# Four chunks of 264 columns in place of three of 352 in a hybrid attention layer's projections

## The chip, the cores and the metric

The kernel runs on one core of a Trainium2 chip. The metric is the device time of one execution in microseconds. Besides the timed runs there is one profiled execution, whose trace gives the start and duration of each instruction on each engine: TensorE (PE, with its weight loads as PEld), VectorE (DVE), ScalarE (ACT), GpSimd (POOL) and the DMA queues.

## What is computed

One layer of a streaming encoder, for 1024 new frames and 32 frames of a running stream (1056 columns in all), with a model width of 1024 in float32. Cut to what matters:

```
u  = rmsnorm(x) @ w_in                       # eleven slices: gq gk gv gr gg dq dk dv dg ma mb
o_gla  = gated linear attention, 4 heads     # gq gk gv and the decay from gr
o_diff = p1 @ v - lam * p2 @ v, 8 heads      # two softmaxes over rotated dq, dk; v = dv
yg = rmsnorm(o_gla)  * silu(gg)
yd = rmsnorm(o_diff) * (1 - lambda_init) * silu(dg)
merged = sigmoid(ma) * (yg @ w_proj_gla) + sigmoid(mb) * (yd @ w_proj_diff)
y = x + rmsnorm(merged @ w_out)
```

Returned are y, the new rows of k and v, and the new linear-attention states, each for the new frames and for the running stream.

## The kernel before

Every float32 operand is split into a high and a low part, and a product is three matmuls: high by high, low by high, high by low. The kernel goes through these stages, in this order of time.

Values (to 214 us): x is normed, and the slices gv and dv are made with 512 columns at a time.

Linear attention (240 to 600 us) and softmax attention (600 to 1183 us): all other slices of the input projection are made here, with features in the rows and the 1056 frames in the columns. Such a projection is a job: 128 output features, whose 128 x 1024 weights are loaded by DMA, rounded to the high part on ACT (L433) and split on POOL (L435). A job works in chunks of columns. A chunk takes one of two banks of the kind `pj` and runs 8 x 3 matmuls into it (L465 to L467); then ACT or DVE reads the bank out: a tanh into a gate (L484), a tanh and a product for a SiLU (L477, L478), a copy into q or k of a linear head (L496) or of a softmax head (L806). There are 56 such jobs. They are the filling work: the attention heads' own steps come first wherever their inputs are there, and the jobs fill the time between.

What comes when on TensorE is set before the program runs by a small planner (class `Order`). Each thread of work yields steps with a cost in us, the events that it needs with a latency, and the banks that it takes. The planner goes through time, always takes the first thread in its list whose step is ready, and writes that step's matmuls. The filling thread yields a step every two of the eight k (six matmuls). On the other engines the scheduler orders the work, and evacuations are placed early (`high_priority`).

First merge (1183 to 1286 us): yg @ w_proj_gla, eight jobs. Two are written by hand in L1087 to L1109 and hold six banks at once, three chunks each; the other six go through the filling thread, with the evacuation L1082 on DVE. Meanwhile DVE scales the softmax heads' results.

Second merge (1286 to 1378 us): yd @ w_proj_diff, eight jobs by `proj` (L443 to L445), each chunk followed by L1152, L1153 and L1155 on DVE and L1154 on ACT.

Output (1378 us to the end): merged @ w_out in four quarters of 256 columns (L1193 to L1195), the last norm and the stores.

Of the kernel before, what the change touches and what calls it, by code (L numbers as in the profile page):

```python
# [23 lines left out]
T = NP + NS  # L24
# [6 lines left out]
EPS = 1e-6  # L31
WC = 352
CHUNKS = [(c * WC, WC) for c in range(T // WC)]
TAU = 16.0
GATE_LIM = 60.0
LAM_INIT = 0.8 - 0.6 * math.exp(0.0)
# [12 lines left out]
N = {"fin": 1, "rr": 3, "q": 2, "k": 4, "fill": 2, "first": 200, "evac": 1200, "lead": 2}  # L49
# [73 lines left out]
def hybrid_step_kernel(ctx: ExitStack, tc: tile.TileContext, a):  # L123
# [15 lines left out]
    def bank(name):  # L139
        return pp.tile([P, 512], F32, tag="pj", bufs=2, name=name)  # L140
# [134 lines left out]
    def value_mm(i, wh, wl, meanwhile=lambda: None):  # L275
        ps = bank("ps_v")
        if i == NQ:
            sample_mm(ps, xsm, wh, wl)
            return ps
        t0 = i * P  # L280
        for k in range(KT):
            if k == 2:
                meanwhile()
            xk = xs[k]
            mm(ps, xk[:, 0, t0 : t0 + P], wh[:, k, :], start=(k == 0), stop=False)  # L285
            mm(ps, xk[:, 1, t0 : t0 + P], wh[:, k, :], start=False, stop=False)  # L286
            mm(ps, xk[:, 0, t0 : t0 + P], wl[:, k, :], start=False, stop=(k == KT - 1))  # L287
        return ps
# [22 lines left out]
    def gate_rank(wgs):  # L311
        for t0, n in CHUNKS:
            ps = bank("ps_gr")
            for k in range(KT):
                mm(ps[0:48, :n], wgs[:, k, :], xs[k][:, 0, t0 : t0 + n], start=(k == 0), stop=(k == KT - 1))
                if k < KT - 1:
                    mm(ps[0:16, :n], wgs[:, k, 0:16], xs[k][:, 1, t0 : t0 + n], start=False, stop=False)
                if k == KT - 2:
                    mm(ps[0:16, :n], wgs[:, k + 1, 0:16], xs[k + 1][:, 1, t0 : t0 + n], start=False, stop=False)
            g1 = v1.tile([16, WC], F32, tag="xr", bufs=2, name="g1")  # L320
            act(g1, ps[32:48, :n], AF.Copy)
            g2 = v1.tile([16, WC], F32, tag="xr", bufs=2, name="g2")
            ve.tensor_tensor(g2, ps[0:16, :n], g1, op=ALU.add)
            act(gst[0:16, t0 : t0 + n], g2, AF.Copy)
            act(gst[64:80, t0 : t0 + n], g2, AF.Copy)
            ve.tensor_tensor(gst[32:48, t0 : t0 + n], g2, gst[0:16, t0 : t0 + n].bitcast(F32), op=ALU.subtract)
# [3 lines left out]
    with tc.manual_schedule(engines={E.PE, E.Activation, E.DVE, E.Pool}):  # L330
# [25 lines left out]
        ps = bank("ps_v")  # L356
# [17 lines left out]
        for i in range(1, NQ + 1):  # L374
# [10 lines left out]
            ps = value_mm(i, *wv, meanwhile)  # L385
# [43 lines left out]
    def wtile(b):  # L429
        wr = wp.tile([P, KT, P], F32, tag="wr", bufs=1, name="wr")  # L430
        dma(wr, a["w128"][b])
        wh = odd(wp, KT, P, tag="wh", name="wh")
        act(wh, wr, AF.Copy)  # L433
        wl = odd(wp, KT, P, tag="wl", name="wl")
        nc.gpsimd.tensor_tensor(wl, wr, wh.bitcast(F32), op=ALU.subtract)  # L435
        return wh, wl

    def proj(w, src, evac):
        wh, wl = w
        for t0, n in CHUNKS:  # L440
            ps = bank("ps_w")
            for k in range(KT):
                mm(ps[:, :n], wh[:, k, :], src[k][:, 0, t0 : t0 + n], start=(k == 0), stop=False)  # L443
                mm(ps[:, :n], wl[:, k, :], src[k][:, 0, t0 : t0 + n], start=False, stop=False)  # L444
                mm(ps[:, :n], wh[:, k, :], src[k][:, 1, t0 : t0 + n], start=False, stop=(k == KT - 1))  # L445
            evac(ps[:, :n], slice(t0, t0 + n))

    def fill(jobs, src):

        w = wtile(jobs[0][0])  # L450
        for ji, (b, event, begin, needs) in enumerate(jobs):
            wh, wl = w
            evac = done = None
            for t0, n in CHUNKS:
                ps = None
                for k in range(KT):
                    if k % N["fill"] == 0:
                        yield 0.45 * N["fill"], (needs if ps is None else []), (["pj"] if ps is None else [])
                        if evac is None:
                            if ji + 1 < len(jobs):  # L460
                                w = wtile(jobs[ji + 1][0])
                            evac, done = begin()
                        if ps is None:
                            ps = bank("ps_w")
                    mm(ps[:, :n], wh[:, k, :], src[k][:, 0, t0 : t0 + n], start=(k == 0), stop=False)  # L465
                    mm(ps[:, :n], wl[:, k, :], src[k][:, 0, t0 : t0 + n], start=False, stop=False)  # L466
                    mm(ps[:, :n], wh[:, k, :], src[k][:, 1, t0 : t0 + n], start=False, stop=(k == KT - 1))  # L467
                with tc.high_priority(offset=N["evac"]):
                    evac(ps[:, :n], slice(t0, t0 + n))
                S.free("pj", W["w_pj"])  # L470
            done()
            S.mark(event)
# [32 lines left out]
    def gla_prep(h):  # L505
# [3 lines left out]

        for t0, n in CHUNKS:  # L510
            yield 0.15, [], ["s"]
# [20 lines left out]
        fl = gp.tile([1, 1], I32, tag="fl", name="fl")  # L532
        ve.tensor_scalar(fl, f1, -TAU * GATE_LIM, None, op0=ALU.is_lt)
        S.free("t", W["pf_t"])
        act(t1, b, AF.Exp, scale=1.0 / TAU)
        ve.tensor_scalar(t2, b, -TAU * GATE_LIM, None, op0=ALU.max)
        act(t2, t2, AF.Exp, scale=-1.0 / TAU)
        yield 0.05, [(("q", h), W["gq"]), (("k", h), W["gk"])], []
# [36 lines left out]
    def gla_exact(h):  # L575
# [3 lines left out]
        with tc.If(flag > 0):  # L579
            for li, half in enumerate(LEVELS + [0]):  # L580
                mask = gp.tile([P, P], F32, tag="sm", name="mask")
                dma(mask, a["masks"][li])
                if half:
# [6 lines left out]
                    for dst, i0, i1, src in ((e1, bv, ref, q), (e2, ref, bv, k)):  # L590
                        dv = dst[:, :ncol].rearrange("p (c s) -> p c s", s=blk)
                        ve.tensor_tensor(dv, i0, i1, op=ALU.subtract)
                        ve.tensor_scalar(dst[:, :ncol], dst[:, :ncol], 0.0, None, op0=ALU.min)
                        act(dst[:, :ncol], dst[:, :ncol], AF.Exp, scale=1.0 / TAU)
                        ve.tensor_tensor(dst[:, :ncol], dst[:, :ncol], src[:, :ncol], op=ALU.mult)
# [13 lines left out]
    def gla_head(h):  # L609
# [9 lines left out]
        bv = b[:, 0:NP].rearrange("p (c s) -> p c s", s=P)  # L619
        act(eb[:, 0:8], bv[:, :, P - 1], AF.Exp, scale=1.0 / TAU)  # L620
        act(eb[:, 8:9], b[:, T - 1 : T], AF.Exp, scale=1.0 / TAU)
# [133 lines left out]
    with tc.manual_schedule(engines=PE):  # L755
        left = S.run([[gla_thread(), None, first], [prep_thread(), None, nullcontext],
                      [fill(jobs, xs), None, nullcontext]],
                     until=lambda: ("on", GH - 1, 1) in S.at and jobs[-1][1] in S.at)
# [279 lines left out]
    for h in range(-1, DH):  # L1038
        need = [(("qk", h - 1), 0.0)] if h >= 1 else []
        n = GATES_DIFF[h + 1]  # L1040
# [8 lines left out]
    with tc.manual_schedule(engines=PE):  # L1049
        left = S.run(left + [[diff_main(), None, first], [sample_thread(), None, nullcontext],  # L1050
                             [fill(jobs, xs), None, nullcontext]],
                     until=lambda: ("pv", DH - 1, 3) in S.at and jobs[-1][1] in S.at)
# [27 lines left out]
    def pg_evac(j):  # L1080
        def evac(ps, sl):
            ve.scalar_tensor_tensor(tha[j][:, sl], tha[j][:, sl], 1.0, ps, op0=ALU.add, op1=ALU.mult)  # L1082
        return evac

    def pg_first():
# [5 lines left out]
        for j, k in sorted(((j, k) for j in range(2) for k in range(KT)), key=lambda e: (e[1] + N["lead"] * e[0], e[0])):  # L1091
# [4 lines left out]
            wh, wl = w[j]  # L1096
            for n, (t0, cw) in enumerate(CHUNKS):
                ps = b[j * 3 + n]
# [3 lines left out]
            if k == KT - 1:  # L1102
                with tc.high_priority(offset=N["evac"]):
                    for n, (t0, cw) in enumerate(CHUNKS):
                        pg_evac(j)(b[j * 3 + n][:, :cw], slice(t0, t0 + cw))
# [38 lines left out]
    for j in range(KT):  # L1144
        th = ld("thb")
        dma(th, thd[1, j])
        pt = ld("ptl")
        dma(pt, ptd[j])
        y = yp.tile([P, 2, T], F32R, tag=f"y{j}", name=f"m{j}")

        def evac(ps, sl, th=th, pt=pt, y=y):
            ve.scalar_tensor_tensor(th[:, sl], th[:, sl], 1.0, ps, op0=ALU.add, op1=ALU.mult)  # L1152
            ve.tensor_tensor(pt[:, sl], pt[:, sl], th[:, sl], op=ALU.add)  # L1153
            act(y[:, 0, sl], pt[:, sl], AF.Copy, scale=0.5)  # L1154
            ve.scalar_tensor_tensor(y[:, 1, sl], pt[:, sl], 0.5, y[:, 0, sl].bitcast(F32), op0=ALU.mult, op1=ALU.subtract)  # L1155
        proj(wtile(BLK_PD + j), yd, evac)
        mg.append(y)
# [26 lines left out]
    for u in range(4):  # L1184
        wh, wl = cw[u]
        csl = slice(u * 256, u * 256 + 256)
        for i in range(NQ + 1):
            t0 = i * P
            w = P if i < NQ else NS
            ps = (bank, dbank)[i % 2]("ps_c")[:, 0:256]  # L1190
# [110 lines left out]
```

## Time and profile before

| what | value |
|---|---|
| median of three runs | 1486.3 us (1482.65 to 1487.47) |
| profiled execution | 1483.59 us, its span 1481.9 us |
| TensorE matmuls | 8848 records, busy 1422.6 us (96%) |
| DVE, ACT, POOL busy | 786.6 us, 601.0 us, 298.4 us |
| mean granted clock of TensorE | 0.99 |

Matmuls are pipelined: one starts long before the other has ended, and their ends are modelled. So the distance between the starts of two neighbours tells what one costs, and the busy time doesn't. A row of a group gives the line, the engine, the operation, output and inputs, the shape and the count, then busy time and mean duration, then the idle time just before and what ended it. A row of a timeline gives the start, the duration and, in brackets, the idle time before and its releaser.

### The profile page before, as it was taken

Reading aid. Unit: us, or ns where it says so; the run is one execution under the profiler, and the core shown is the slowest. Engines: PE = TensorE matmul, PEld = TensorE weight load, DVE = VectorE, ACT = ScalarE, POOL = GpSimd, SP = SyncE. Lnnn points to the kernel's source line nnn. Section 1 sums busy time; section 2 is a strip of 40 time slices with the busy share of each in tenths; the row PEclk is TensorE's granted clock in tenths of the full one; section 3 lists DMA queues with packets and bytes.
Section 4 is the critical chain, followed back from the end, with each engine's and each line's share of the span. In section 5 each row is a group of like instructions: output and inputs, shape, how many; then the busy total and the mean of one; then the engine's idle time right before and its main releaser. Section 6 shows DMA issues by size and latency. Waiting matters only on the chain.

```text
span 1481.9 us, 22365 instructions
## 1 busy us (share of the span) xinstructions
PE 1422.6 (96%) x8848; PEld 1327.6 (90%) x8848; DVE 786.6 (53%) x1464; ACT 601.0 (41%) x1262; POOL 298.4 (20%) x186
## 2 busy tenths in 40 slices
PE   8999999989999999899999999999899899999997
PEld 6787789889989899899989998998899799999997
DVE  5702005755565343576767767678665535455415
ACT  5612114535344232455555555555455432221311
POOL 1200002222213224123222222222221111122001
PEclk9999999999999999999999999999999999999999
DMA  8621111122222233323232333223322278633205
GB/s 310 205 105 38 45 45 48 56 74 68 81 70 73 70 120 108 90 62 106 72 108 60 106 86 96 69 83 90 92 68 81 97 264 302 223 131 129 103 1 192
DMA packets 66742, 156.58 MB, mean 106 GB/s; under 512 B 10008, under 2 KB 28568, under 8 KB 65600
## 3 DMA queue, kind: packets, MB, share of 16 engines
q1 hardware_dynamic: 66624, 155.01, 32.3%
q8 instruction: 74, 1.21, 0.3%
q14 instruction: 44, 0.36, 0.1%
HBM read 104.39 MB, written 40.04 MB: 97 GB/s over the span
## 4 chain that ended last, share of the span: by engine, by line
PE 51%; DVE 6%; DMA 4%; ACT 2%; issue 1%; POOL 1%; SPq 0%; DVEq 0%; POOLq 0%; ACTq 0%
PE ps_w L465 9%; PE ps_w L466 9%; PE ps_w L467 9%; PE ps_w L444 2%; PE ps_w L443 2%; PE ps_w L445 2%; PE ps_s L884 2%; PE ps_t L931 2%; PE ps_s L883 2%; DMA ydr<-ydd 2%; PE ps_c L1193 2%; PE ps_c L1195 2%; PE ps_c L1194 2%; PE po L945 1%; PE po L946 1%
## 5 line engine op out<-in xcount | busy, mean ns | idle before, releaser
L465 PE MATMUL ps_w<-X,wh 128*128 128x352 f32 x1344 | 453.8, 338 | 8.5 <-DVE sg L478 3.2
L466 PE MATMUL ps_w<-X,wl 128*128 128x352 f32 x1344 | 438.2, 326 | 0.0
L467 PE MATMUL ps_w<-X,wh 128*128 128x352 f32 x1344 | 436.4, 325 | 0.0
L435 POOL TENSOR_TENSOR wl<-wr,wh 128x1024 fp32r<-128x1024 f32 x72 | 179.5, 2493 | 661.8 <-ACT wh L433 528.6
L465 PEld LDWEIGHTS ps_w<-X,wh 128*128 128x128 f32 x1344 | 255.8, 190 | 13.6 <-issue 4.9
L466 PEld LDWEIGHTS ps_w<-X,wl 128*128 128x128 f32 x1344 | 256.1, 191 | 1.2 <-issue 1.2
L467 PEld LDWEIGHTS ps_w<-X,wh 128*128 128x128 f32 x1344 | 255.1, 190 | 0.0
L889 ACT ACTIVATE p<-ps_s,nm 128x256 f32<-128x256 f32 (+7 forms) x128 | 94.6, 741 | 59.1 <-DVE ps_s L885 31.1
L286 PE MATMUL ps_v<-wh,X 128*128 128x512 f32 x248 | 97.6, 393 | 0.6 <-DVE X L225 0.6
L287 PE MATMUL ps_v<-wl,X 128*128 128x512 f32 x248 | 98.0, 395 | 0.0
L433 ACT ACTIVATE wh<-wr 128x1024 fp32r<-128x1024 f32 x72 | 75.9, 1054 | 54.6 <-PE ps_w L467 30.4
L285 PE MATMUL ps_v<-wh,X 128*128 128x512 f32 x248 | 97.9, 395 | 0.0
L887 DVE TENSOR_REDUCE nm<-ps_s 128x1 f32<-128x256 f32 (+7 forms) x128 | 94.8, 747 | 2.7
L272 DVE TENSOR_TENSOR vo<-ps_v,vo 32x512 f32<-32x512 f32 x4 | 2.7, 679 | 139.9 <-ACT vo L271 139.9
L885 DVE MEMSET ps_s<- 64x64 f32 x128 | 14.3, 112 | 115.8 <-PE ps_s L884 114.2
L650 POOL TENSOR_TENSOR vl<-vr,vh 128x512 fp32r<-128x512 f32 (+1 forms) x20 | 24.8, 1242 | 222.8 <-DVE t L516 160.3
L883 PE MATMUL ps_s<-k,q 128*128 128x512 f32 (+2 forms) x192 | 68.0, 362 | 1.2 <-DMA k<-k 1.2
L884 PE MATMUL ps_s<-kl,q 128*128 128x512 f32 (+2 forms) x192 | 63.8, 348 | 3.9 <-DMA kl<-kl 3.4
L268 ACT ACTIVATE vo<-ps_v 128x512 f32<-128x512 f32 x32 | 19.1, 596 | 114.2 <-PE ps_v L287 113.8
L933 ACT ACTIVATE ah<-ps_t 128x512 fp32r<-128x512 f32 (+2 forms) x96 | 46.9, 488 | 43.6 <-PE ps_t L931 43.0
L934 DVE TENSOR_TENSOR al<-ps_t,ah 128x512 fp32r<-128x512 f32 (+2 forms) x96 | 53.1, 554 | 18.6 <-ACT ah L933 17.3
L444 PE MATMUL ps_w<-Y,wl 128*128 128x352 f32 x192 | 62.2, 324 | 0.0
(319 smaller groups left out, 2960.9 us busy)
## 6 DMA issues: line engine op xcount, KB each, us to landing
wr<-w SPq DMA_DIRECT2D x72, 512.0 KB
thd<-gate SPq DMA_DIRECT2D x16, 528.0 KB
xn<-xn SPq DMA_DIRECT2D x16, 512.0 KB
wr<-wv SPq DMA_DIRECT2D x16, 512.0 KB
newk<-rr SPq DMA_DIRECT2D x8, 528.0 KB
ygr<-ygd SPq DMA_DIRECT2D x8, 528.0 KB
tha<-thd SPq DMA_DIRECT2D x8, 528.0 KB
ydr<-ydd SPq DMA_DIRECT2D x8, 528.0 KB
```

The source lines that it names most:

```text
L285: mm(ps, xk[:, 0, t0 : t0 + P], wh[:, k, :], start=(k == 0), stop=False)
L286: mm(ps, xk[:, 1, t0 : t0 + P], wh[:, k, :], start=False, stop=False)
L287: mm(ps, xk[:, 0, t0 : t0 + P], wl[:, k, :], start=False, stop=(k == KT - 1))
L435: nc.gpsimd.tensor_tensor(wl, wr, wh.bitcast(F32), op=ALU.subtract)
L444: mm(ps[:, :n], wl[:, k, :], src[k][:, 0, t0 : t0 + n], start=False, stop=False)
L465: mm(ps[:, :n], wh[:, k, :], src[k][:, 0, t0 : t0 + n], start=(k == 0), stop=False)
L466: mm(ps[:, :n], wl[:, k, :], src[k][:, 0, t0 : t0 + n], start=False, stop=False)
L467: mm(ps[:, :n], wh[:, k, :], src[k][:, 1, t0 : t0 + n], start=False, stop=(k == KT - 1))
L883: mm(ps[:, n0 : n0 + n], qs[m][:, qsl], ks[m][:, n0 : n0 + n], start=True, stop=False)
L884: mm(ps[:, n0 : n0 + n], qs[m][:, qsl], kls[m][:, n0 : n0 + n], start=False, stop=True)
L887: ve.tensor_reduce(nm, ps[:, 0:w], axis=AX.X, op=ALU.max, negate=True)
L889: act(p[:, 0:w], ps[:, 0:w], AF.Exp, bias=nm, accum_out=sm[:, m : m + 1])
```

## The change

A second list of chunks is added, four of 264 columns, and used in three places: in `proj` (the second merge), in the filling thread (all 56 jobs of the two attention stages and six jobs of the first merge), and in the planner's cost of a filling step, which becomes 0.35 us for each k where it was 0.45. The old list stays in use for the gate's rank projection, for the linear heads' decay, and for the two jobs of the first merge that are written by hand. Evacuations take the width from the chunk.

```diff
 WC = 352
 CHUNKS = [(c * WC, WC) for c in range(T // WC)]
+
+NC = 264
+COLS = [(c * NC, NC) for c in range(T // NC)]
@@
     def proj(w, src, evac):
         wh, wl = w
-        for t0, n in CHUNKS:
+        for t0, n in COLS:
             ps = bank("ps_w")
@@
             evac = done = None
-            for t0, n in CHUNKS:
+            for t0, n in COLS:
                 ps = None
                 for k in range(KT):
                     if k % N["fill"] == 0:
-                        yield 0.45 * N["fill"], (needs if ps is None else []), (["pj"] if ps is None else [])
+                        yield 0.35 * N["fill"], (needs if ps is None else []), (["pj"] if ps is None else [])
```

Line numbers of the changed kernel are three higher than before from here on.

The order of ACT's work in the first head of linear attention, before. L535, L620, L621 and L537 are exponentials of the head's summed decay, L496 reads out a chunk of q or k, L433 rounds weights.

```order
L496 ACTIVATE q<-ps_w 128x352
L433 ACTIVATE wh<-wr 128x1024
L535 ACT_TABLE_LOAD
L535 ACTIVATE t_1481<-b 128x1056
L620 ACTIVATE eb<-b 128x8
L621 ACTIVATE eb<-b 128x1
L537 ACTIVATE t_1482<-t_1482 128x1056
L496 ACTIVATE k<-ps_w 128x352
L545 ACTIVATE qh<-t_1481 128x1056
L496 ACTIVATE k<-ps_w 128x352 x2
```

The same place in the changed kernel:

```order
L499 ACTIVATE q<-ps_w 128x264
L436 ACTIVATE wh<-wr 128x1024
L538 ACT_TABLE_LOAD
L538 ACTIVATE t_1481<-b 128x1056
L623 ACTIVATE eb<-b 128x8
L624 ACTIVATE eb<-b 128x1
L540 ACTIVATE t_1482<-t_1482 128x1056
L499 ACTIVATE k<-ps_w 128x264
L548 ACTIVATE qh<-t_1481 128x1056
L499 ACTIVATE k<-ps_w 128x264 x3
```

The first chunk of k stands behind the same exponentials in both; it is smaller, and three follow it in place of two.

The order of TensorE's work at the end of softmax attention, before. L931 are transposes of the last head, L944 to L946 its last products, L1006, L1018, L1019 and L1029 belong to the running stream's frames, L1099 to L1101 are the first merge.

```order
L1006 MATMUL ps_st<-ident,p 32x128
L1018 MATMUL po_s<-vcs,smp 32x128 x4
L1019 MATMUL po_s<-smp 32x128
L931 MATMUL ps_t<-ident,p 128x128 x8
L1018 MATMUL po_s<-vcs,smp 32x128 x4
L1019 MATMUL po_s<-smp 32x128
L944 MATMUL po<-ah,vh 128x256
...
L946 MATMUL po<-ah,vl 128x128
L1029 MATMUL ps_so<-ident,os__13006 128x64
L1099 MATMUL ps_w<-y_13072,wh 128x352
```

In the changed kernel, from the last product of the last head on (L862 sums its squares):

```order
L949 MATMUL po<-ah,vl 128x128
L1009 MATMUL ps_st<-ident,p 128x128 x4
L468 MATMUL ps_w<-X_88,wh 128x264
...
L862 MATMUL ps_m<-sqo,one_h 128x512
L1009 MATMUL ps_st<-ident,p 32x128
L468 MATMUL ps_w<-X_89,wh 128x264
...
L862 MATMUL ps_m<-sqo,one_h 128x512
L470 MATMUL ps_w<-X_89,wh 128x264
L1102 MATMUL ps_w<-y_14528,wh 128x352
```

The last head's products come before the end of the filling work now, so 18 matmuls of it and two sums stand between them and the merge; the two groups of four transposes, which were one row of eight, have 24 matmuls of filling work between them.

## The prediction

> **What bounds the kernel now.** I read the page first, then the busy time by stage, then the starts of single matmuls.
>
> ```profile
> span 1481.9 us, 22365 instructions
> PE 1422.6 (96%) x8848; PEld 1327.6 (90%) x8848; DVE 786.6 (53%) x1464; ACT 601.0 (41%) x1262; POOL 298.4 (20%) x186
> PE 51%; DVE 6%; DMA 4%; ACT 2%; issue 1%; POOL 1%; SPq 0%; DVEq 0%; POOLq 0%; ACTq 0%
> ```
>
> TensorE is busy nearly all the time and holds most of the chain that ended last. The profiled execution took 1483.6 us around its span of 1481.9; the median of the runs is 1486.3, which is 2.7 more. The sum below is made against 1483.6, and 2.7 is added at its end.
>
> ```profile
> core 0: us, PE busy (x) PEld busy (x) DVE busy (x) ACT busy (x) POOL busy (x), PEclk, DMA share, GB/s
> 240.00:600.00 360.00, 339.46 (x2173) 325.99 (x2173) 186.47 (x312) 146.66 (x295) 97.19 (x57) 0.99 0.26 80
> 600.00:1183.00 583.00, 565.76 (x3628) 534.89 (x3628) 395.25 (x784) 301.65 (x695) 140.02 (x66) 0.99 0.28 84
> 1213.00:1285.60 72.60, 70.77 (x434) 69.19 (x433) 35.72 (x39) 18.07 (x19) 14.59 (x6) 1.00 0.75 269
> 1285.60:1378.30 92.70, 92.70 (x578) 92.70 (x577) 47.07 (x71) 19.59 (x32) 18.61 (x14) 1.00 0.39 131
> ```
>
> These are the stages that the change touches: the linear-attention stage (240 to 600), the softmax-attention stage (600 to 1183), the rest of the first merge (1213 to 1286) and the second merge (1286 to 1378). In each TensorE leaves little open and DVE and ACT have room. So what counts first is how far apart the starts of two matmuls lie, then the few places where TensorE waits.
>
> A matmul's own duration (338 ns on the page) overlaps its neighbours', so I take the distance of starts, where nothing else runs between. The rows give an operation, its count, its durations, and its first and last start.
>
> ```profile
> L443 PE MATMUL ps_w<-Y,wh x192: 318/323/326, 1285.7 to 1377.9; 128*128 128x352 f32 x192
> L1193 PE MATMUL ps_c<-cwh,m x64: 276/276/284, 1378.4 to 1399.8; 128*128 128x256 f32 x64
> L1193 PE MATMUL ps_c<-C,m x64: 281/282/285, 1402.0 to 1424.5; 128*128 128x256 f32 x64
> L1193 PE MATMUL ps_c<-C,m x64: 276/276/276, 1426.7 to 1448.1; 128*128 128x256 f32 x64
> L1193 PE MATMUL ps_c<-C,m x64: 276/276/276, 1450.2 to 1471.7; 128*128 128x256 f32 x64
> ```
>
> L443 is the first of three matmuls of 352 columns: 92.2 us over 191 triples is 482.7 ns a triple, 160.9 ns a matmul. L1193 is the first of three of 256 columns: 21.4 us over 63 triples is 113.2 ns a matmul in the first and third quarter of that stage, 113.8 in the fourth, and 22.5 us gives 119.0 in the second. Same shape, same stage, other tiles: where the operands lie moves a matmul of 256 columns by 6 ns. Per column that is 0.442 to 0.465 ns; the 352 wide ones take 0.457.
>
> **The matmuls.** How many there are:
>
> ```profile
> L465 PE MATMUL ps_w<-X,wh 128*128 128x352 f32 x1344 | 453.8, 338 | 8.5 <-DVE sg L478 3.2
> L465 PE MATMUL ps_w<-y,wh 128*128 128x352 f32 x144 | 47.1, 327 | 1.8 <-DVE tha L1082 1.8
> ```
>
> With the 192 of L443 this is 1680, in three passes and three chunks, so 1680 groups of three matmuls of 352 columns (5040) become 1680 groups of four of 264 (6720). The columns stay the same. Break-even is 482.7 / 4 = 120.7 ns a matmul.
>
> No row has 264 columns. From below: the best 256 wide pace by the column, 113.2 x 264/256 = 116.7 ns. From above: the worst, 119.0 x 264/256 = 122.7. In money: 4 x 116.7 - 482.7 = -15.9 ns x 1680 = -26.7 us; 4 x 122.7 - 482.7 = +8.1 ns x 1680 = +13.6 us. Weight loads could be a floor under this:
>
> ```profile
> 703.69 0.19 PEld L945 LDWEIGHTS po<-al,vh 128*128 128x128 f32 x1
> 703.80 0.19 PEld L946 LDWEIGHTS po<-ah,vl 128*128 128x128 f32 x1
> 703.91 0.19 PEld L465 LDWEIGHTS ps_w<-X,wh 128*128 128x128 f32 x1
> ```
>
> Behind matmuls of 128 columns they follow each other at 110 ns, so 264 columns still cover one, by 7 ns at the best pace. I take 119.5 ns, near the middle of the two ends since 264 is nearer to 256 than to 352 and half-way between good and bad tiles: 478.0 - 482.7 = -4.7 ns x 1680 = **-7.9 us**, between -26.7 and +13.6.
>
> The Trainium skill, TensorE: Matmul & The Clock Gate, section Back-to-back issue gap, gives N / 2.4 + 2.5 ns between matmuls at full clock, so every matmul pays a fixed 2.5. By it 352 columns take 149.2 and 264 take 112.5, and the group grows by 2.4 ns: an estimate of +4 us where I have -7.9. The trace puts 352 columns at 160.9, so the size of the rule isn't met here; its sign is a rival below.
>
> **Late evacuations.** A chunk's bank is one of two, and it comes free when ACT (or DVE) has read it. Two chunks cover a late one: 7.72 us of matmuls now, 48 x 119.5 ns = 5.74 after. In the first head of linear attention that cover is too short already:
>
> ```profile
> 229.92 0.32 PE L465 MATMUL ps_w<-X,wh 128*128 128x352 f32 x1
> 237.47 0.32 PE L467 MATMUL ps_w<-X,wh 128*128 128x352 f32 x1
> 240.95 0.66 PE L465 MATMUL ps_w<-X,wh 128*128 128x352 f32 x1 [3.16 <-ACT k L496]
> 231.03 5.89 DVE L524 TENSOR_TENSOR_SCAN b<-ones,t 128x128 f32<-128x128 f32 x9
> 237.00 1.28 ACT L535 ACT_TABLE_LOAD   x1 [5.46 <-DVE b L524]
> 240.45 0.44 ACT L496 ACTIVATE k<-ps_w 128x352 f32<-128x352 f32 x1
> 240.90:244.30 3.40, 3.35 (x12) 3.35 (x13) 1.26 (x1) 1.32 (x2) 0.00 (x0) 0.56 0.00 0
> PE ps_w L465 <- ACT k L496: 3.2, 1, 3.2
> PE ps_w L465 <- DVE sg L478: 3.2, 3, 1.9
> ```
>
> The job k starts at 229.9, fills two banks by 237.6, and waits until ACT, which sat behind an exponential that waits for nine scans on DVE, reads the first. With 264 columns the two banks are full at 235.7 while ACT is free at the same time: 2.0 us more. Behind the waiting matmul in TensorE's queue stands the rest of job k, and the head's score products wait for that. The last two rows are the waits view of 214 to 600: four such waits, 6.4 us. A wait that begins in a bank's first chunk grows by two chunks' difference (2.0), in its second by one (1.0). So four waits cost +2 (the first alone) to +8, and as many that just fit now could appear, up to +14. I take **+7**. The row of 240.90 shows the clock at 0.56 for the 3.4 us behind that stall; a stall longer than that is inside the +14.
>
> **Switches and ACT's work.** When TensorE comes back from transposes to the filling work, its first matmul takes longer:
>
> ```profile
> 920.42 0.41 PE L465 MATMUL ps_w<-X,wh 128*128 128x352 f32 x1
> 920.67 0.32 PE L466 MATMUL ps_w<-X,wl 128*128 128x352 f32 x1
> 920.83 0.32 PE L467 MATMUL ps_w<-X,wh 128*128 128x352 f32 x1
> ```
>
> 0.25 us to the next start, not 0.16. The order of TensorE leaves the filling work 232 times before and 247 times after (the step is shorter): 15 x 0.09 = **+1.3 us**, 0 to +2. Evacuations are more and shorter:
>
> ```profile
> L484 ACT ACTIVATE gate<-ps_w 128x352 f32<-128x352 f32 x48 | 22.2, 462 | 61.7 <-PE ps_w L467 61.6
> L947 ACT ACTIVATE sqo<-po 128x256 f32<-128x256 f32 x32 | 12.2, 380 | 41.3 <-PE po L946 38.1 <-issue 3.2
> ```
>
> Three of 462 ns become four of about 387 (an estimate between both rows): 0.16 us a job, 9 us of ACT over the 56 jobs of the two attention stages, where matmuls run beside it and ACT is busy half the time. I cost it at nothing; were none of it hidden, it would be +9. The weights' DMAs and their conversion stay one to a job. The planner's cost of a step (0.70 us for six matmuls, where 6 x 119.5 is 0.72; it was 0.90 for 0.97) puts dependent steps 4% closer in real time; 0, between -5 and +5.
>
> **The end of softmax attention.** The new order places the last head earlier against the filling work, as the rows of TensorE's order show. Now:
>
> ```profile
> 1174.38 0.66 PE L931 MATMUL ps_t<-ident,p 128*128 128x128 f32 x4
> 1176.45 0.66 PE L931 MATMUL ps_t<-ident,p 128*128 128x128 f32 x4 [1.41 <-DVE al L934]
> 1183.47 0.43 PE L1099 MATMUL ps_w<-y,wh 128*128 128x352 f32 x1 [1.51 <-ACT y L1069]
> 1184.99 0.43 PE L1101 MATMUL ps_w<-y,wh 128*128 128x352 f32 x1 [0.93 <-DVE y L1070]
> 1191.24 0.43 PE L1101 MATMUL ps_w<-y,wh 128*128 128x352 f32 x1 [0.63 <-DVE y L1070]
> ```
>
> Eight transposes follow each other with the one bank between them, and the first merge starts right behind the last products, whose tiles its own inputs need. That is 4.5 us of waits. After, a chunk of 24 matmuls (2.9 us) stands between the two groups of transposes, and 18 matmuls and two sums stand before the merge. I take **-4**, between -4.5 and 0.
>
> **Sum.** -7.9 + 7 + 1.3 - 4 = -3.6: 1480.0 for the profiled execution, 1482.7 for the median.
>
> **The rivals.** (1) Good tiles. All paces lie near the lower end, 117.2 ns: 468.8 - 482.7 = -13.9 ns x 1680 = -23.4, with the other terms (+4.3) -19: 1467. For it: three of the four quarters of L1193 run at 113.2 to 113.8. Against it: the 352 wide matmuls, whose tiles are the ones read here, do not reach 0.442 ns a column.
>
> (2) A fixed cost per matmul: slower. By the best column, 352 x 0.442 = 155.7 ns; the measured 160.9 is 5.2 more. If these 5.2 belong to each matmul of this kind, whatever its width, then 264 x 0.442 + 5.2 = 121.9, 4.9 ns over a group, +8.2 us, and with +4.3: 1498.8. It decides from 120.7 ns on. For it: the excess sits on these operands. Against it: 256 wide ones have three quarters with none. The page named above has such a fixed cost, of 2.5.
>
> (3) The banks: slower. If not four but ten evacuations come too late, in the linear stage and in the first merge where DVE's scaling stands before them, ten times 2.0 is +20 in place of 7: -7.9 + 20 + 1.3 - 4 = +9.4, 1495.7. It decides from about six such waits of 2 us each. Against it: in the softmax stage chunks are broken up by other steps, so their cover is longer.
>
> **How the numbers follow.** My forecast has 0.40, with 1478 to 1489 as its own range; (1) 0.22, (2) 0.25, (3) 0.13. About 0.3% (4.5 us) is what a measurement of this kernel can tell from no change. The forecast lies near that border: 0.20 of it counts as faster, 0.16 as no change, 0.04 as slower. With (1) all faster, (2) 0.22 slower and 0.03 the same, (3) 0.09 slower and 0.04 the same, it is faster 0.42, same 0.23, slower 0.35. The range of 1464 to 1503 takes in (1), (2) and (3) and leaves out both ends of the pace together with their worst waits.
>
> **What would show it.** In the second merge L443 has 256 rows from first to last start: 91.4 us at 119.5 ns, 92.3 at break-even, 93.3 at 121.9. The wait on the evacuation of k in the first head: 5 us, not 3.2. The waits of the first merge on y: under 1 us, and none between the last transposes. A pace over 122.7 or under 116.7, or a new wait of more than 5 us in the softmax stage, makes the prediction wrong.

## The result and the profile after

The changed kernel is slower: 1561.2 us, median of four runs (1553.2 to 1562.22), where the kernel before takes 1485.8 beside it (four runs, 1482.65 to 1487.47). The ratio is 1.050, with an interval of 1.047 to 1.054. The forecast was 1482.7 with a range up to 1503, so the time lies far outside it. The profiled executions show the same: a span of 1551.4 us against 1481.9, 69.5 more. The profiled execution is the quickest of the changed kernel; the others took 1561 to 1562 us at a mean clock of 0.969 to 0.973 where it had 0.978, so its trace shows 69.5 of the 75 us.

The head of the page of the changed kernel, its shares of the chain that ended last, and one of its costliest groups:

```profile
span 1551.4 us, 25835 instructions
PE 1448.4 (93%) x10528; PEld 1353.1 (87%) x10528; DVE 792.3 (51%) x1510; ACT 607.9 (39%) x1326; POOL 302.6 (20%) x186
PE 47%; DVE 9%; DMA 4%; ACT 3%; issue 2%; POOL 1%; SPq 0%; DVEq 0%; POOLq 0%; ACTq 0%
L887 PE MATMUL ps_s<-kl,q 128*128 128x512 f32 (+2 forms) x192 | 65.3, 354 | 23.6 <-DMA kl<-kl 23.6
```

TensorE was busy 96% of the span and is busy 93% now, while DVE's and ACT's busy times rose by 6 and 7 us only. So no other engine has become the bound; TensorE stands still more often. The last row tells the main place: L887 is the second of the products that make a softmax head's scores, it reads kl, the low part of the rounded k, and it had to wait 23.6 us in all until a DMA had brought kl.

Where the time went by stage. These are the two attention stages, the first merge and the second merge of the changed kernel; a row gives the window, its length, the busy time (and count) of PE, PEld, DVE, ACT and POOL, the granted clock, the DMA share and GB/s:

```profile
240.00:1252.00 1012.00, 927.66 (x7104) 883.95 (x7104) 583.30 (x1113) 456.39 (x1044) 236.26 (x120) 0.97 0.25 77
1252.00:1354.40 102.40, 98.86 (x743) 95.32 (x742) 48.45 (x59) 32.17 (x37) 21.54 (x9) 1.00 0.74 268
1354.40:1447.50 93.10, 93.10 (x767) 93.10 (x767) 53.73 (x97) 20.77 (x41) 18.59 (x14) 1.00 0.41 133
```

The first two of these stages in the kernel before (the prediction shows the third):

```profile
240.00:1183.40 943.40, 905.22 (x5801) 860.87 (x5801) 582.12 (x1096) 448.70 (x991) 237.21 (x122) 0.99 0.27 82
1183.40:1285.60 102.20, 98.12 (x580) 94.17 (x581) 47.90 (x52) 31.46 (x33) 16.98 (x7) 0.98 0.75 266
```

The two merges take what they took (102.4 for 102.2, 93.1 for 92.7). Of the 69.5 us, 68.6 lie in the attention stages: 1012.0 for 943.4. There TensorE's open time went from 38.2 to 84.3 us, which is 46 more, and its busy time rose by 22. The matmuls' own pace is some 5 us of that (below); the rest fits the clock, which was granted at 0.97 there and had been at 0.99, but was not measured apart.

What ended TensorE's waits, in the changed kernel (total us, times, the longest):

```profile
PE ps_s L887 <- DMA kl<-kl: 23.6, 12, 4.0
PE ps_t L934 <- DVE ps_s L888: 9.6, 5, 2.2
PE ps_kt L636 <- DVE k L628: 9.1, 4, 2.7
PE po L703 <- DVE o_sb L712: 7.6, 8, 2.1
PE ps_s L886 <- DMA k<-k: 6.0, 4, 2.5
PE ps_w L468 <- DVE sg L481: 5.6, 3, 2.1
PE ps_w L468 <- ACT k L499: 4.7, 1, 4.7
PE ps_w L468 <- ACT q L499: 1.9, 1, 1.9
PE ps_w L468 <- DVE tha L1085: 1.6, 2, 1.0
```

The same waits before (those on sg and k are in the prediction):

```profile
PE po L700 <- DVE o_sb L709: 4.1, 5, 1.5
PE ps_s L884 <- DMA kl<-kl: 3.4, 3, 2.2
PE ps_w L465 <- DVE tha L1082: 1.8, 4, 0.9
PE ps_kt L633 <- DVE k L625: 1.8, 2, 1.2
PE ps_s L883 <- DMA k<-k: 1.2, 1, 1.2
PE ps_t L931 <- DVE ps_s L885: 0.9, 3, 0.3
```

The wait on k's and kl's DMA grew from 4.6 to 29.6 us, 25 of the 46. Then come the transposes behind a head's scores (L934, +8.7), the transposes of k in the linear heads (L636, +7.3), evacuations (8.2 to 13.8, +5.6) and the linear heads' products (L703, +3.5). Only the evacuations are waits that the prediction had its eye on; the other four of the five stand outside the filling work that was changed.

One softmax head shows the largest. The row of ACT is the evacuation of the head's last chunk of k, the first row of PE its first score product. Changed kernel:

```profile
913.18 0.39 ACT L809 ACTIVATE rr<-ps_w 128x264 f32<-128x264 f32 x1 [0.23 <-PE ps_w L470]
927.63 1.17 SPq L842 DMA_DIRECT2D k<-k  x2
928.89 0.58 SPq L842 DMA_DIRECT2D kl<-kl  x1
930.88 0.44 PE L886 MATMUL ps_s<-k,q 128*128 128x128 f32 x1 [2.46 <-DMA k<-k]
933.20 0.45 PE L887 MATMUL ps_s<-kl,q 128*128 128x128 f32 x1 [1.88 <-DMA kl<-kl]
933.45 0.41 PE L886 MATMUL ps_s<-k,q 128*128 128x128 f32 x1
937.00 0.44 PE L887 MATMUL ps_s<-kl,q 128*128 128x128 f32 x1 [3.14 <-DMA kl<-kl]
```

The same head before:

```profile
861.38 0.46 ACT L806 ACTIVATE rr<-ps_w 128x352 f32<-128x352 f32 x1 [0.17 <-PE ps_w L467]
880.16 1.17 SPq L839 DMA_DIRECT2D k<-k  x2
881.42 1.67 SPq L839 DMA_DIRECT2D kl<-kl  x2
888.49 0.27 PE L883 MATMUL ps_s<-k,q 128*128 128x128 f32 x1
888.60 0.27 PE L884 MATMUL ps_s<-kl,q 128*128 128x128 f32 x1
```

Before, k's DMA was issued 18.8 us behind the evacuation and the last of kl's by 883.1; the first score came at 27.1 us, and TensorE waited for neither. Now TensorE's order has it some 15 us behind; k is normalised, rotated, rounded and brought by DMA at 17.7 us, the first part of kl at 20.0 and the next at 23.8, and TensorE waits for each of them. The planner counts this way at 14.32 us (its latency `W["dk"]`). That figure was too short before as well, as the 18.8 us show. It mattered little, because the heads from the second on ran so far behind the jobs that feed them that other work stood between; only the first head stood 15 us behind, and it waited 3.4 us.

### The profile page after: what moved, and what is told of

Read it like the earlier page. It is cut to its first block, busy times and chain, and to the rows that moved or that the text cites. A ratio compares the mean times of both kernels' runs of the same rounds, so it can differ in the third digit from the quotient of the medians.

```text
span 1551.4 us, 25835 instructions
## 1 busy us (share of the span) xinstructions
PE 1448.4 (93%) x10528; PEld 1353.1 (87%) x10528; DVE 792.3 (51%) x1510; ACT 607.9 (39%) x1326; POOL 302.6 (20%) x186
## 4 chain that ended last, share of the span: by engine, by line
PE 47%; DVE 9%; DMA 4%; ACT 3%; issue 2%; POOL 1%; SPq 0%; DVEq 0%; POOLq 0%; ACTq 0%
PE ps_w L468 8%; PE ps_w L469 8%; PE ps_w L470 8%; DMA kl<-kl 2%; PE ps_w L447 2%; PE ps_w L448 2%; PE ps_w L446 2%; PE ps_t L934 2%; PE ps_s L887 2%; PE ps_s L886 2%; PE ps_c L1196 1%; PE ps_c L1198 1%; PE ps_c L1197 1%; DVE p L896 1%; PE ps_m L862 1%
## 5 line engine op out<-in xcount | busy, mean ns | idle before, releaser
L468 PE MATMUL ps_w<-X,wh 128*128 128x264 f32 x1792 | 535.2, 299 | 12.3 <-DVE sg L481 5.6
L470 PE MATMUL ps_w<-X,wh 128*128 128x264 f32 x1792 | 516.4, 288 | 0.0
L469 PE MATMUL ps_w<-X,wl 128*128 128x264 f32 x1792 | 515.6, 288 | 0.0
L468 PEld LDWEIGHTS ps_w<-X,wh 128*128 128x128 f32 x1792 | 345.1, 193 | 18.2 <-DVE sg L481 6.2
L469 PEld LDWEIGHTS ps_w<-X,wl 128*128 128x128 f32 x1792 | 345.0, 193 | 2.8 <-issue 2.7
L470 PEld LDWEIGHTS ps_w<-X,wh 128*128 128x128 f32 x1792 | 344.0, 192 | 0.2 <-issue 0.2
L887 PE MATMUL ps_s<-kl,q 128*128 128x512 f32 (+2 forms) x192 | 65.3, 354 | 23.6 <-DMA kl<-kl 23.6
L448 PE MATMUL ps_w<-Y,wh 128*128 128x264 f32 x256 | 72.8, 284 | 0.0
L447 PE MATMUL ps_w<-Y,wl 128*128 128x264 f32 x256 | 72.7, 284 | 0.0
L446 PE MATMUL ps_w<-Y,wh 128*128 128x264 f32 x256 | 72.5, 283 | 0.0
```

The source lines that it names most:

```text
L887: mm(ps[:, n0 : n0 + n], qs[m][:, qsl], kls[m][:, n0 : n0 + n], start=False, stop=True)
```

## The experiments

All of them compute everything. In what follows A is the theory that the order costs the time: by the planner's new numbers the heads' steps find their turn sooner, catch up with their inputs, and waits and half clock (a granted clock of 0.5) follow. B is the rival that the narrow chunks themselves cost it: their matmuls, evacuations and banks. Each kernel ran beside the kernel before, which took 1484.9 to 1486.4 us in these groups.

**The planner's cost alone, two ways.** First the changed kernel, with a job as long in the planner as it had been (10.8 us in place of 11.2):

```diff
-                        yield 0.35 * N["fill"], ...
+                        yield 0.3375 * N["fill"], ...
```

> The changed kernel with four chunks of 264, but a planner's cost of 0.3375 us for each k in place of 0.35, so that a whole job has the cost it had before (10.8 us). Theory A (the planner's order brings each softmax head's scores too close behind the job that makes its k): in this order 25 to 27 us of TensorE work lie between the last matmul of a head's k job and the head's first score, as before, where the changed kernel has 15.6 from the fourth head on; the waits on the DMA of k all but vanish and the time falls to 1495 to 1510 (before + 7 for the matmuls, + some 5 to 15 for late evacuations). Theory B (the narrower matmuls and the smaller banks cost the time themselves): nothing that they do has changed, 1550 to 1565.

Measured: 1516.4 us, ratio 1.020 (1.019 to 1.022). Less than 4% of a number in a table, with the same chunks and matmuls, gives back 45 of the 75 us. The heads' scores come 25 to 26 us behind k's job again, and the wait on kl falls:

```profile
PE ps_s L887 <- DMA kl<-kl: 4.7, 4, 2.9
PE ps_kt L636 <- DVE k L628: 7.3, 4, 2.1
```

So most of the loss isn't the chunks. Nor is it the shorter step by itself: the step is 0.675 us here, shorter still than 0.70. The time stayed above what A had said, and 31 us were still to be explained.

The same cost on the kernel before, a job of 11.2 us there:

```diff
-                        yield 0.45 * N["fill"], ...
+                        yield 0.4667 * N["fill"], ...
```

> The kernel before with three chunks of 352, and a planner's cost of 0.4667 us for each k in place of 0.45, so that a whole job costs the planner 11.2 us as in the changed kernel. Theory A, if the dearer job alone moves the scores up: waits on the DMA of k as in the changed kernel. In this order, however, the distance stays at 25 to 26 us, so by A the time stays within 10 us of before: 1480 to 1496. Theory B: the same, 1480 to 1495. It tells whether the dearer job or the shorter step moves the heads.

Measured: 1500.7 us, ratio 1.010 (1.008 to 1.012), a little beyond what was expected. The linear heads lose here, as in the changed kernel:

```profile
PE ps_kt L633 <- DVE k L625: 9.4, 4, 4.6
```

It was 1.8 before. The longer job costs about 15 us when alone. It doesn't explain this wait in the changed kernel (9.1), since with the job back at 10.8 us it was still 7.3, as shown above. And the heads stay 24 to 26 us behind k's job, so the longer job alone doesn't move them.

**The step's length alone.** The kernel before, wide chunks, with steps of one k (0.45 us) in place of two:

```diff
-    "fill": 2
+    "fill": 1
```

> The kernel before with three chunks of 352 and its planner's cost, but a filling step of one k (three matmuls) in place of two. Theory A: in this order the distance between a head's k job and its first score falls to 15.4 to 15.6 us from the fourth head on, as in the changed kernel, without any chunk of 264; waits on the DMA of k of 20 us or more, and 1525 to 1560. Theory B: no width changes, 1480 to 1495.

Measured: 1552.1 us, ratio 1.045 (1.043 to 1.047), as A expected. Not one matmul or evacuation differs from the kernel before, and the loss is nearly that of the changed kernel, with the same waits:

```profile
PE ps_s L884 <- DMA kl<-kl: 23.1, 13, 3.2
PE ps_s L883 <- DMA k<-k: 9.5, 4, 3.2
```

The heads stand 15 to 16 us behind k's job here. So steps of 0.45 us in a job of 10.8 move them, and steps of 0.70 in a job of 11.2; steps of 0.675 in a job of 10.8 don't, nor steps of 0.93 in a job of 11.2. No single number of the planner was shown to decide it: the order that comes of all of them does.

**Order and width apart.** The filling thread was written so that the chunks and the planner's steps no longer hang together. First the wide chunks in the order of the changed kernel, sixteen steps of 0.70 us and four turns of a bank, and wide chunks in `proj` too:

```diff
+            units = [(t0, n, k) for t0, n in CHUNKS for k in range(KT)]
...
+            for s in range(16):
+                head = s % 4 == 0
+                yield 0.7, (needs if head else []), (["pj"] if head else [])
...
+                upto = ((s + 1) * len(units) + 16 // 2) // 16
+                for t0, n, k in units[at:upto]:
...
```

> The opposite: chunks of 352, as before, in the order of the changed kernel: the planner sees 16 steps of 0.70 us a job and four bank turns, and each step writes one or two k of the three chunks. Only the order changes. Theory A: waits on the DMA of k of 20 us or more, 1535 to 1560. Theory B: 1480 to 1495.

Measured: 1556.4 us, ratio 1.048 (1.044 to 1.052). The order, with the old chunks, costs nearly as much as the change:

```profile
PE ps_s L892 <- DMA kl<-kl: 21.2, 12, 3.1
PE ps_s L891 <- DMA k<-k: 8.8, 4, 2.7
```

Then the narrow chunks in the order of the kernel before, twelve steps of 0.90 us, each with two or three k:

```diff
+            units = [(t0, n, k) for t0, n in COLS for k in range(KT)]
...
+            for s in range(12):
+                head = s % 4 == 0
+                yield 0.9, (needs if head else []), (["pj"] if head else [])
...
+                upto = ((s + 1) * len(units) + 12 // 2) // 12
...
```

> Chunks of 264 in the order of the kernel before: the planner sees 12 steps of 0.90 us a job and three bank turns, as before, and each step writes two or three k of the four chunks (8/3 on average). So only the width of the matmuls and the size of what a bank holds change. Theory A (the order makes the loss, the width costs 7 us for the matmuls and some us for evacuations that come too late): 1490 to 1503, with waits on the DMA of k under 6 us. Theory B (width and banks make it): 1545 to 1565.

Measured: 1511.0 us, ratio 1.017 (1.015 to 1.020). That is 26 us with the order kept, more than A had allowed the width. Its waits on evacuations are 17.6 us (8.2 before):

```profile
PE ps_w L470 <- DVE sg L486: 8.1, 7, 1.9
PE ps_w L470 <- DVE tha L1090: 4.8, 4, 1.7
PE ps_w L470 <- ACT k L504: 4.7, 1, 4.7
```

The two don't add: 26 and 72 alone, 75 together. In both kernels a chunk's bank turns also fall in other places of a step than the planner counts, so neither is a pure change; the steps of one k above, where they don't, lose nearly as much.

**The narrow chunks where no planner is.** The kernel before, with four chunks of 264 in `proj` alone, so in the second merge:

```diff
     def proj(w, src, evac):
-        for t0, n in CHUNKS:
+        for t0, n in [(c * 264, 264) for c in range(4)]:
```

> The kernel before, with four chunks of 264 in the second merge alone, where no planner sets the order. Theory A: the matmuls' pace there is that of the changed kernel, 121.6 ns, so 192 groups cost 192 x (4 x 121.6 - 482.7) = +0.7 us and nothing else changes: 1484 to 1488, no change that can be told. Theory B (the width costs time by itself): the second merge holds 8 of the 70 jobs, so a loss of 75 us that went with the jobs would show as +8 to +9, 1493.

Measured: 1487.5 us, ratio 1.001 (0.999 to 1.003): no difference, and B's loss isn't there in this stage. The first matmul of a triple in the second merge, in this kernel and then in the changed one:

```profile
L443 PE MATMUL ps_w<-Y,wh x256: 278/284/291, 1286.4 to 1379.5; 128*128 128x264 f32 x128
```

```profile
L446 PE MATMUL ps_w<-Y,wh x256: 278/284/289, 1354.5 to 1447.5; 128*128 128x264 f32 x128
```

93.0 us over 255 triples is 121.6 ns a matmul.

**Can the latencies be mended?** If the short `W["dk"]` were all, a true one would bring the time back. The changed kernel with 22 us:

```diff
-    "dk": 14.32
+    "dk": 22.0
```

> The changed kernel with one number more changed: the latency that the planner takes from the end of a k job to its scores is 22.0 us in place of 14.32. Theory A: the distance becomes 23 us or more, the waits on the DMA of k (29.6 us in the changed kernel) fall under 5, the transposes' waits fall with them, and the time falls by 25 to 50, to 1510 to 1535. Theory B: 1550 to 1565, since matmuls and banks are as they were.

Measured: 1541.9 us, ratio 1.038 (1.036 to 1.040). The wait on kl is gone, and only 19 us with it; A had expected 26 to 51. Others took its place:

```profile
PE ps_s L887 <- DMA kl<-kl: 1.7, 1, 1.7
PE ps_w L1102 <- ACT y L1072: 6.9, 1, 6.9
PE ps_so L1032 <- DVE os__13039 L1028: 4.0, 1, 4.0
```

The first merge now waits for the last head's result, which fits heads that stand further back (22 to 27 us behind k's job). Next the narrow chunks with the cost of the job, the latency of k and that of the linear heads' decay all mended together:

```diff
-                        yield 0.35 * N["fill"], ...
+                        yield 0.3375 * N["fill"], ...
-    "kd": 3.96      "dk": 14.32
+    "kd": 7.0       "dk": 20.0
```

> Chunks of 264 with the planner's cost of 0.3375 us for each k, and two of the planner's latencies nearer to what the changed kernel's trace shows: from a linear head's decayed keys to their transposes 7.0 us in place of 3.96, from a k job to its scores 20.0 in place of 14.32. Theory A: the waits of the transposes on the decayed keys (7.3 us with this cost and the old latencies) and on the DMA of k (4.7) go, and the time is 1495 to 1512, below the 1516 without the two latencies. If the order is only good or bad by chance, it can be anywhere from 1495 to 1550.

Measured: 1534.7 us, ratio 1.034 (1.031 to 1.038): 18 us slower than with the cost alone. The waits that the latencies were to take away are gone, those on k's DMA and the 7.3 us of the linear heads' transposes on `k`, but the same transposes now wait 12.6 us on `kdl`, from 1.9. The forecast of 1495 to 1512 failed. Then latencies nearer to the truth in the kernel before:

```diff
-    "kd": 3.96      "dk": 14.32
+    "kd": 5.0       "dk": 20.0
```

> The kernel before with two of the planner's latencies changed: 5.0 us in place of 3.96 from the decayed keys to their transposes, and 20.0 in place of 14.32 from a k job to its scores. If longer latencies were all that an order needs, it would be a little faster than before, 1478 to 1485 (2.4 us of waits on k in the first softmax head go). If the numbers fit together only as they stand, 1490 to 1530.

Measured: 1511.4 us, ratio 1.018 (1.015 to 1.021): the waits on k's DMA are gone, and 26 us are lost. To take away the 4.6 us that the kernel before waits for k, one smaller step:

```diff
-    "dk": 14.32
+    "dk": 17.0
```

> The kernel before with the latency from a k job to its scores at 17.0 us in place of 14.32, nothing else. The first softmax head's waits on k (3.4 us) should go. If that is all, 1481 to 1485; if any other order than the present one loses time elsewhere, as with 20 us (1511), 1487 to 1505.

Measured: 1514.9 us, ratio 1.020 (1.018 to 1.022), slower than either expectation. The wait on kl fell by half a microsecond, and the transposes behind the scores lost 17:

```profile
PE ps_t L931 <- DVE ps_s L885: 13.1, 5, 3.3
PE ps_t L931 <- DVE al L934: 8.5, 7, 1.6
```

**Longer steps.** The changed kernel with four k (1.40 us) to a step:

```diff
-    "fill": 2
+    "fill": 4
```

> The changed kernel with a filling step of four k (twelve matmuls) in place of two, at the same planner's cost of a k. Theory A (a shorter step lets the heads catch up with the jobs that feed them): in this order 27 to 40 us lie between a head's k job and its scores, waits on the DMA of k stay under 6 us, and the time is under the changed kernel's 1561, at 1500 to 1540; how far under depends on what the coarser step delays elsewhere. Theory B: 1550 to 1565.

Measured: 1526.1 us, ratio 1.027 (1.024 to 1.029): the heads fall back to 33 to 40 us behind their k, the wait on kl is 2.9 us, and 35 of the 75 us come back, with waits on evacuations and on `al` in place of the rest.

**Side by side.** The second column is the TensorE work between the end of k's job and the head's first score, for softmax heads 3 to 7: the matmuls between them, each at the middle distance of starts of its form. The fourth adds up, over the whole trace, by how much the distance to the next matmul's start exceeds the middle one of its form, where by more than 30 ns (a form is a line and a shape); it holds the waits and the slow matmuls at half clock.

| kernel | scores behind k's job, us | waits on k and kl, us | stalls, us | mean clock | span, us |
|---|---|---|---|---|---|
| before | 25 to 27 | 4.6 | 107 | 0.990 | 1481.9 |
| changed | 15 to 16 | 29.6 | 165 | 0.978 | 1551.4 |
| wide, steps of one k | 15 to 16 | 32.6 | 176 | 0.971 | 1550.0 |
| wide, order of the changed | 15 to 16 | 30.0 | 180 | 0.969 | 1554.8 |
| wide, cost 0.4667 | 24 to 26 | 5.7 | 123 | 0.987 | 1498.9 |
| wide, k 17 | 26 to 30 | 2.9 | 134 | 0.986 | 1513.0 |
| wide, k 20, kd 5 | 32 to 34 | 0 | 128 | 0.983 | 1508.4 |
| narrow, order of before | 25 to 27 | 6.3 | 124 | 0.984 | 1510.0 |
| narrow, cost 0.3375 | 25 to 26 | 4.9 | 129 | 0.981 | 1516.0 |
| narrow, k 22 | 22 to 27 | 1.7 | 154 | 0.978 | 1539.4 |
| narrow, cost 0.3375, k 20, kd 7 | 28 to 33 | 0 | 146 | 0.979 | 1533.8 |
| narrow, steps of four k | 33 to 40 | 3.1 | 138 | 0.982 | 1526.0 |

Against the kernel before, the stalls grew by 69, 73, 16, 27 and 21 us in the five wide kernels, and their spans by 68, 73, 17, 31 and 27: the stalls are nearly the whole of it. In the six narrow ones the spans grew by 10 to 13 us more than the stalls, of which the matmuls' pace gives 6 (below). The rest is too small per place to be put down to anything here. The three kernels whose heads stand 15 to 16 us behind k's job are those at 1550 to 1555, with some 30 us of waits on k. A longer distance takes these waits away but doesn't bring back the time: the other kernels lie between 1499 and 1539.

What stays open. Every change of the order that was tried on the wide chunks, in either direction, lost between 15 and 72 us against the present one. That the present order is a narrow optimum, to which its untrue latencies belong, fits all of these runs, but why each single one loses was not settled; after every mended wait another stood up elsewhere.

## Why the prediction was wrong, step by step

**What bounds the kernel**: right. TensorE's pace and its waits set the time, and no other engine became the bound.

**The matmuls**: sign wrong. The second merge has 93.0 us for 255 triples, which is 121.6 ns a matmul; I took 119.5, break-even was 120.7, and the rival with a fixed cost had 121.9. Over 1680 groups that is 4 x 121.6 - 482.7 = 3.7 ns, +6.2 us and not -7.9; the attention stages show 121 to 122 ns as well. By the column it is 0.461 ns, as poor as 352 wide ones at 0.457 on the same kind of tiles, and not half-way to the best 256 wide ones at 0.442. The point that I held against the fixed cost, that other stages' 256 wide matmuls have none, was evidence from other tiles, and it was circular, since the 0.442 was their whole pace divided by their width. The row on these tiles spoke for a fixed cost, and I weighed it too little. The two widths on the same tiles now give it: 88 columns make 39.3 ns, so 0.447 ns a column and 3.7 ns a matmul (an estimate from two points). The Trainium skill, TensorE: Matmul & The Clock Gate, section Back-to-back issue gap, gives the formula that the prediction used for a single matmul by itself, and not for a stream with a weight load to each. Here it had the sign right and, with 112.5 and 149.2 ns for the two widths, both sizes too low.

**Late evacuations**: right. They grew from 8.2 to 13.8 us, +5.6 for +7. The one in the first linear head was to go from 3.2 to 5 and went to 4.7:

```profile
239.47 0.28 PE L470 MATMUL ps_w<-X,wh 128*128 128x264 f32 x1
244.45 0.39 PE L468 MATMUL ps_w<-X,wh 128*128 128x264 f32 x1 [4.69 <-ACT k L499]
244.20:247.60 3.40, 3.15 (x15) 3.15 (x16) 1.30 (x2) 1.45 (x3) 0.00 (x0) 0.59 0.00 0
```

The last row is the window of 3.4 us behind it, at a clock of 0.59: a wait costs more than its own length. I had left that inside the upper end, for this one wait. Ten late evacuations, as in the third rival, are not what happened.

**ACT's extra work**: right at nothing. ACT is busy 7.7 us longer in the attention stages (456.4 for 448.7), near the 9 of the estimate, and it became nobody's bound. **Switches**: the size is right and the count isn't. Behind transposes the first matmul of the filling work takes 85 ns longer in both kernels (246 for 161 ns before, 206 for 122 after), but that is at 94 places where it was 90, so +0.3 us and not +1.3.

**The end of softmax attention**: right. Between the last transposes there is no wait now, and the first merge waits 1.2 us on y where it had waited 3.1 (under 1 was forecast). This was -4 in the sum and is about -3.

**The planner's cost and the order**: this is the step that failed. I wrote that a step of 0.70 for 0.72 where it was 0.90 for 0.97 "puts dependent steps 4% closer in real time; 0, between -5 and +5". What I compared was how true the cost is. What decided is what the planner makes of its numbers: the heads came to stand 15 to 16 us behind the jobs that feed them, where the latency of 14.32 us lets them in, and k takes 17.7 to 23.8 us. That order, with the old chunks, costs 72 us. Why just these numbers give it stays open, since neither the shorter step nor the longer job does so alone. I had read in the new order that the last head comes earlier against the filling work, and booked it as a gain at the end, without asking what the same shift does to each head's inputs at its start. The order could be read before the result: 25 to 27 us of TensorE work between k's job and the scores became 15 to 16, and the trace before has k's DMA issued only 18.8 us behind the job. "A new wait of more than 5 us in the softmax stage" was named as what would make the prediction wrong; it came, as twelve waits on kl of up to 4 us, 23.6 in all.

So the terms that were costed come to about 6 + 6 - 3 = +9 us, inside the range. Of the 69.5 us between the spans that leaves some 60, at the one place that was put at nothing. It is a remainder and not a measured share of the order: the order costs 72 us with the wide chunks, the narrow chunks cost 26 in the old order, and the two don't add.

## What to carry to other kernels

Where a planner writes the order before the program runs, a change of the costs in its table is a change of its own, apart from the work in the step: compare for each consumer how much work stands between it and its producer in the old and the new order, and set that against what the trace shows the producer's whole way to take, the DMA's landing with it. A latency in such a table that is too short shows nothing as long as something else keeps the consumer back, and mending it alone moves the trouble on. Time a change of tile size and a change of order in separate kernels before they are put together.

## What the hardware showed that was not expected

Half clock came behind a stall of 2.46 us. In the head shown above TensorE waits 2.46, 1.88 and 3.14 us with one or two matmuls between; the same stretch in windows of the changed kernel:

```profile
929.50:932.90 3.40, 0.44 (x1) 0.28 (x1) 2.62 (x2) 1.52 (x4) 3.40 (x3) 0.71 0.70 181
930.40:933.80 3.40, 1.04 (x3) 0.78 (x3) 2.40 (x3) 0.62 (x1) 3.40 (x3) 0.57 0.51 146
933.00:936.40 3.40, 0.66 (x2) 0.50 (x2) 0.40 (x2) 0.46 (x2) 2.13 (x1) 0.50 0.85 241
936.40:939.80 3.40, 2.79 (x7) 1.79 (x8) 1.26 (x5) 0.95 (x3) 0.00 (x0) 0.50 0.89 299
```

The clock is 1.00 up to 930.0, and 0.50 still in the last row, where the matmuls run again. Full clock until 930.9 and half from there gives the 0.71 and the 0.57 of the first two rows (an estimate), so it fell right at the end of the first stall, of 2.46 us. The Trainium skill, TensorE: Matmul & The Clock Gate, section HAM oscillation — how this bites in real kernels, gives the rule to leave no gap of more than about 3.4 us; by this trace a gap of 2.46 us can be enough, so the rule is a little too lenient. The length alone doesn't decide: behind a wait of 2.7 us at 809.7 us of the same trace the clock stays at 1.00. Over the whole span the mean clock fell from 0.990 to 0.978: 1551.4 x 0.022 - 1481.9 x 0.010 is 19 us of full clock more lost, part of it while TensorE waited anyway. The kernels with the most stalls, 180 and 176 us, have the lowest clocks, 0.969 and 0.971.

And a matmul's pace by the column is not set by its width alone: 352 columns took 160.9 ns and 264 took 121.6 (0.457 and 0.461 ns a column), while 256 took between 113.2 and 119.0 in one and the same stage. What makes the quarters of one stage differ was not tried; the places of their tiles are a candidate and no more.
